# Second feed-forward of a two-layer fp32 backbone: first products of the inner tiles 4 to 21 by Strassen's seven block products

## The chip, the core and the metric

One core of one Trainium2 chip runs the whole kernel as one launch. The metric is the device time of a run in microseconds (us), lower is better; the number compared is the median of the runs.

## What is computed

The reference is a backbone of two layers over 512 latent tokens of 1024 channels. The edited part is the feed-forward at the end of the second layer (l = 1), a SwiGLU with 2816 hidden channels:

```
hn  = rms_norm(h) * (1 + scale) + shift        # 512 tokens x 1024 channels
a   = silu(hn @ w1) * (hn @ w3)                # 512 x 2816
h   = h + gate * (a @ w2)                      # 512 x 1024
```

Everything is float32. TensorE multiplies in a shorter form, so each factor x is carried as a high part xh (x rounded to that form) and a low part xl = x - xh, and each product is three matmul passes: xh*yh, xl*yh and xh*yl.

## The kernel before

Channels lie on the 128 partitions, tokens along the free axis. The 2816 hidden channels are 22 tiles of 128 (j = 0 to 21), in three groups, `GROUPS = [(0, 8), (8, 8), (16, 6)]`. `ffn` (L866) does for each group first its tiles and then eight output tiles dt of w2. Tile 0 of a layer comes from `Lead` (L268), begun before the norm is known. For every other tile:

- `Stream.get` (L147) hands out two weight tiles, w1 and w3 of this j, each 128 x 1024 (eight blocks of 128 channels, kt = 0 to 7). `Stream.fill` (L137) loads raw tiles four ahead through SP's queue (`w_r`) and splits them two ahead: ScalarE writes the high part `w_h` (L65, the helper `act`), VectorE the low part `w_l` (L144).
- TensorE runs `passes` (L157 to L161): for each kt and for w1 and w3 three matmuls of 512 columns (all tokens) into the two halves of the PSUM tile `h_ps`: 48 matmuls for a tile. The moving operands `hnh`, `hnl` are the high and low parts of hn, made once from `nrm_u` (L326).
- `si` = Silu of one half (ScalarE), `av` = si times the other half (VectorE, L893), and its split: `ah` (ScalarE), `al` (VectorE, L896).

Then `w_ps`, the product with w2, takes 24 matmuls of 512 columns for a dt (18 in the last group), again in `passes`, and L907 adds it to h. A scheduler sets each engine's order; the PSUM tag of `h_ps` has two slots, the rings of `w_h` and of `w_l` three slots in either of two pools.

Further up in layer 1 the pooling mixer has `z_ps` (L159 to L161 from `pool_z`), a product by matmuls of 256 columns, and `pl_ps` (L996 to L999).

Of the kernel before, what the change touches and what calls it, by code (L numbers as in the profile page):

```python
# [22 lines left out]
GROUPS = [(0, 8), (8, 8), (16, 6)]  # L23
EPS = 1e-6
# [5 lines left out]
def kernel(  # L30
# [92 lines left out]
    class Stream:  # L123
        """Weight tiles in the order of their use: loaded LD tiles and split LS tiles ahead."""

        def __init__(self, units, LD=4, LS=2):
            self.units, self.LD, self.LS, self.raw, self.ready, self.used = units, LD, LS, [], [], 0

        def load(self, n):
            while len(self.raw) < min(n, len(self.units)):  # L130
                src, m = self.units[len(self.raw)]
                self.raw.append(raw_tile(m, "w_r"))
                nc.sync.dma_start(out=self.raw[-1], in_=src)

        def fill(self, used):
            while len(self.ready) < min(used + self.LS, len(self.units)):
                k = len(self.ready)  # L137
                self.load(k + 1)
                n = self.units[k][1]
                pool, t = (wp_, "") if alt["pool"] is None or k % 2 == 0 else (alt["pool"], "2")  # L140
                hi = pool.tile([P, n], F32R, tag="whi" + t, bufs=3, name="w_h")
                act(hi, self.raw[k])
                lo = pool.tile([P, n], F32R, tag="wlo" + t, bufs=3, name="w_l")
                nc.vector.tensor_tensor(lo, self.raw[k], f32(hi), op=ALU.subtract)  # L144
                self.ready.append((hi, lo))
            self.load(used + self.LD)

# [32 lines left out]
    class AdaCols:  # L180
        """Modulation columns [l][t]: each a product with the broadcast condition, summed along the free axis."""
# [24 lines left out]
    class Norm:  # L206
        """Statistics of an RMS norm, one 128-channel tile at a time."""
# [22 lines left out]
        def rstd_cols(self, ps=None):  # L230
            """One column per 128 tokens, which lie on the partitions."""
            if ps is None:
                ps = mm.tile([P, 512], F32, tag="mm", name="nrm_ps")
            nb = self.n // P
            for m, src_ in enumerate(self.parts):
                for b in range(nb):
                    nc.tensor.matmul(ps[:, b:b + 1], src_[:, b * P:(b + 1) * P], ones[:, 0:1],
                                     start=(m == 0 and b == 0), stop=(m == len(self.parts) - 1 and b == nb - 1))
            std = cp.tile([P, nb], F32, tag="stdc", bufs=2, name="std")
            act(std, ps[:, 0:nb], AF.Sqrt, scale=1.0 / D, bias=eps)  # L240
            rs = cp.tile([P, nb], F32, tag="stdc", bufs=2, name="rs")
            nc.vector.reciprocal(out=rs, in_=std)
            return rs
# [80 lines left out]
    def norm_apply(pool, src, n, rstd, A, B, hi, lo, late=None):  # L324
        u = pb.tile([P, n], F32, tag="tmp", bufs=8, name="nrm_u")
# [18 lines left out]
    def ffn_units(l):  # L344
        u = []
        for gi, (j0, nj) in enumerate(GROUPS):
            for j in range(j0, j0 + nj):
                u += [(w1[l, j], 1024), (w3[l, j], 1024)]
            u += [(w2a[l, gi, dt] if gi < 2 else w2b[l, dt], nj * P) for dt in range(KT)]
        return u  # L350
# [7 lines left out]
    # =============== layer 0: mixer ===============  # L358
    with ExitStack() as es:
# [354 lines left out]
        def attn_out(i, jp, st):  # L714
            """Two heads of either kv group on 128 tokens: probabilities turned and multiplied with the values."""
# [200 lines left out]
    bh = pf.tile([P, 4, 536], F32R, tag="bh", bufs=1, name="bh")  # L916
    bl = pf.tile([P, 4, 16], F32R, tag="bl", bufs=1, name="bl")
# [39 lines left out]
    G1 = cp.tile([P, KT], F32, name="G1")  # L957
    nc.vector.tensor_tensor(G1, ada[1][:, 16:24], g_sb[:, 5, :], op=ALU.mult)
    nrm = Norm(pf, T, sq=("sq", 4, "sqa", 1), eng=nc.gpsimd, direct=4)
    # 128 rows of tokens: first and last with the columns up to the middle, inner ones with their 144 columns;  # L960
    # the reciprocal counts are powers of two except at 8 columns on either end, so only those have a low part
    spans = ((0, 0, 256, 0, 0, 0), (3, 256, 512, 136, 504, 8), (1, 120, 264, 392, 0, 0), (2, 248, 392, 392, 0, 0))
    def pool_z(g):
# [5 lines left out]
        for half in range(2):  # L969
# [7 lines left out]
            zh, zl = sf("zh", dt=F32R, tag="a", bufs=24), sf("zl", dt=F32R, tag="a", bufs=24)  # L977
# [42 lines left out]
    rstd = ffn(1, rstd, Af1, lead).rstd()  # L1020

# [8 lines left out]
def _host_layout(i):  # L1030
# [48 lines left out]
    # constants of the shapes alone  # L1079
# [46 lines left out]
```

## Time and profile before

| | |
|---|---|
| device time, median of 3 runs | 1021.93 us (1021.84 to 1022.23) |
| span of the profiled execution (its own time, first to last instruction) | 1020.0 us |
| median less that span | 1.9 us |
| mean granted TensorE clock | 0.995 of 2.4 GHz |
| tile 1 of layer 1's feed-forward starts on TensorE | 651.2 us |
| DMA, mean over the span | 136 GB/s |

The page gives busy time by engine and by slice of the span; the trace gives every instruction with its start and length. The start of a matmul is recorded, its end is modelled, so the pace of TensorE is read from start to start. Of layer 1's feed-forward, tiles 1 to 7 lie at 651.2 to 729, the first group's w2 to 773.5, tiles 8 to 15 to 862, the second w2 to 906.5, tiles 16 to 21 to 973 and the last w2 behind them.

### The profile page before, as it was taken

To read this page: it belongs to the slowest core of one execution; us is meant where nothing else is said; L and a number is where in the kernel's file an instruction comes from. 1 tells how busy PE (TensorE), PEld (TensorE's weight loads), DVE (VectorE), ACT (ScalarE), POOL (GpSimd) and SP (SyncE) were. 2 spreads that over 40 slices of the span, in tenths; PEclk is the share of its full clock that TensorE was granted. 3 is DMA by queue.
4 is the path that set the end of the run, shared out by engine and by line. 5 is a ranking of instruction groups with operands and counts; after the bars stand their busy time and mean duration, and the time that the engine had idled before them with its cause. 6 is when DMAs were issued, how large, how long until landed. Compare 5 with 4: busy or idle time off the path is not lost.

```text
span 1020.0 us, 12270 instructions
## 1 busy us (share of the span) xinstructions
PE 987.0 (97%) x4816; PEld 783.4 (77%) x4816; DVE 571.5 (56%) x903; ACT 375.3 (37%) x595; POOL 26.6 (3%) x27
## 2 busy tenths in 40 slices
PE   5999999999999999999999998999999999999995
PEld 3666777776888888888888888788888888888884
DVE  4678667889866455663554498842332233323234
ACT  4568565455523212322222455532222232213231
POOL 1011001011000000000000001000000000000000
PEclk9999999999999999999999999999999999999998
DMA  9830322653777356673465431133323223322202
GB/s 349 317 103 31 104 63 87 221 168 109 227 245 264 115 176 215 218 235 124 148 214 163 136 104 55 62 92 112 97 92 93 94 83 102 105 83 75 90 1 83
DMA packets 44409, 139.15 MB, mean 136 GB/s; under 512 B 5440, under 2 KB 5568, under 8 KB 44352
## 3 DMA queue, kind: packets, MB, share of 16 engines
q1 hardware_dynamic: 44352, 138.38, 41.5%
q8 instruction: 38, 0.62, 0.3%
q14 instruction: 19, 0.16, 0.0%
HBM read 136.26 MB, written 2.10 MB: 136 GB/s over the span
## 4 chain that ended last, share of the span: by engine, by line
PE 89%; DVE 7%; ACT 2%; issue 1%; DMA 0%; DVEq 0%; SPq 0%; ACTq 0%
PE h_ps L159 16%; PE h_ps L161 16%; PE h_ps L160 16%; PE w_ps L161 8%; PE w_ps L159 8%; PE w_ps L160 8%; PE pv_ps L734 2%; PE t_ps L723 1%; PE mo_ps L159 1%; PE mo_ps L161 1%; PE mo_ps L160 1%; PE s_ps L686 1%; PE s_cx L399 1%; DVE w_l L144 1%; PE s_ps L687 1%
## 5 line engine op out<-in xcount | busy, mean ns | idle before, releaser
L65 ACT ACTIVATE w_h<-w_r 128x1024 fp32r<-128x1024 f32 (+2 forms) x158 | 156.4, 992 | 452.0 <-PE h_ps L161 275.4
L144 DVE TENSOR_TENSOR w_l<-w_r,w_h 128x1024 fp32r<-128x1024 f32 (+2 forms) x158 | 181.1, 1148 | 196.7 <-ACT w_h L65 196.3
L159 PE MATMUL h_ps<-hnh,w_h 128*128 128x512 f32 x672 | 265.5, 395 | 0.0
L161 PE MATMUL h_ps<-hnl,w_h 128*128 128x512 f32 x672 | 264.8, 394 | 0.0
L160 PE MATMUL h_ps<-hnh,w_l 128*128 128x512 f32 x672 | 264.1, 393 | 0.4 <-DVE w_l L144 0.4
L160 PEld LDWEIGHTS h_ps<-hnh,w_l 128*128 128x128 f32 x672 | 126.5, 188 | 30.2 <-DVE w_l L144 0.8
L161 PEld LDWEIGHTS h_ps<-hnl,w_h 128*128 128x128 f32 x672 | 126.2, 188 | 29.9
L159 PEld LDWEIGHTS h_ps<-hnh,w_h 128*128 128x128 f32 x672 | 126.2, 188 | 28.7
L161 PE MATMUL w_ps<-al,w_h 128*128 128x512 f32 x352 | 138.3, 393 | 0.0
L159 PE MATMUL w_ps<-ah,w_h 128*128 128x512 f32 x352 | 138.3, 393 | 0.0
L160 PE MATMUL w_ps<-ah,w_l 128*128 128x512 f32 x352 | 138.2, 393 | 0.0
L198 DVE SCALAR_TENSOR_TENSOR ada_r<-ada_r,condB 128x1024 f32<-128x1024 f32 x80 | 97.6, 1222 | 66.0 <-DMA ada_r<-in_adaR_dram 66.0
L907 DVE SCALAR_TENSOR_TENSOR h<-w_ps,ada,h 128x512 f32<-128x512 f32 x48 | 36.0, 751 | 101.5 <-PE w_ps L161 101.5
L160 PEld LDWEIGHTS w_ps<-ah,w_l 128*128 128x128 f32 x352 | 66.3, 188 | 14.8
L161 PEld LDWEIGHTS w_ps<-al,w_h 128*128 128x128 f32 x352 | 66.2, 188 | 14.8
L159 PEld LDWEIGHTS w_ps<-ah,w_h 128*128 128x128 f32 x352 | 66.2, 188 | 14.7
L65 ACT ACTIVATE ah<-av 128x512 fp32r<-128x512 f32 x44 | 27.8, 632 | 41.5 <-DVE av L893 39.0
L65 ACT ACTIVATE sq<-h 128x512 f32<-128x512 f32 x38 | 23.4, 624 | 30.5 <-DVE h L907 19.8
L896 DVE TENSOR_TENSOR al<-av,ah 128x512 fp32r<-128x512 f32 x44 | 30.2, 686 | 0.7 <-ACT ah L65 0.7
L65 ACT ACTIVATE p<-s_ps,nm 128x512 f32<-128x512 f32 (+1 forms) x32 | 23.6, 737 | 15.2 <-DVE nm L695 15.0
L694 DVE TENSOR_REDUCE mx<-s_ps 128x1 f32<-128x512 f32 (+1 forms) x32 | 24.1, 753 | 8.9 <-PE s_ps L691 8.7
L893 DVE TENSOR_TENSOR av<-si,h_ps 128x512 f32<-128x512 f32 x42 | 28.6, 680 | 0.0
(244 smaller groups left out, 1106.6 us busy)
## 6 DMA issues: line engine op xcount, KB each, us to landing
w_r<-in_w_dram SPq DMA_DIRECT2D x88, 512.0 KB, 3.5
ada_r<-in_adaR_dram SPq DMA_DIRECT2D x80, 512.0 KB, 4.2
w_r<-in_w2a_dram SPq DMA_DIRECT2D x32, 512.0 KB, 4.2
ada_q<-in_adaP_dram SPq DMA_DIRECT2D x32, 256.0 KB, 5.4
w_r<-in_w2b_dram SPq DMA_DIRECT2D x16, 384.0 KB, 3.1
w_r<-in_wo_dram SPq DMA_DIRECT2D x16, 256.0 KB, 2.8
wa_r<-in_wa_dram SPq DMA_DIRECT2D x8, 384.0 KB, 5.7
h<-in_xT_dram SPq DMA_DIRECT2D x4, 512.0 KB, 5.4
```

The source lines that it names most:

```text
L65: return nc.scalar.activation(out=out, in_=in_, func=func, **kw)
L144: nc.vector.tensor_tensor(lo, self.raw[k], f32(hi), op=ALU.subtract)
L159: nc.tensor.matmul(acc, wh, mh, start=start, stop=False)
L160: nc.tensor.matmul(acc, wl, mh, start=False, stop=False)
L161: nc.tensor.matmul(acc, wh, ml, start=False, stop=stop)
L198: nc.vector.scalar_tensor_tensor(out=r, in0=r, scalar=1.0, in1=condB, op0=ALU.mult, op1=ALU.mult, accum_out=ada[l][:, t:t + 1])
L399: nc.tensor.matmul(ps[32 * g:32 * g + 32, :], condS[:, kt, :], r[:, k * n:(k + 1) * n], start=(kt < 4), stop=(kt >= 4), tile_position=(0, ...
L694: nc.vector.tensor_reduce(out=mx, in_=sp[:, lo_:hi_], op=ALU.max, axis=AX.X)
L734: nc.tensor.matmul(ops[64 * kv:64 * kv + 64, 0:256], VS[:, kbs[n], kv, :], th[:, 256 * kv:256 * kv + 256], start=(n == 0), stop=(n == N - ...
L893: nc.vector.tensor_tensor(av, si, hp[:, 512:1024], op=ALU.mult)
L896: nc.vector.tensor_tensor(al, av, f32(ah), op=ALU.subtract)
L907: nc.vector.scalar_tensor_tensor(out=h[:, dt, :], in0=acc, scalar=ada[l][:, 40 + dt:41 + dt], in1=h[:, dt, :], op0=ALU.mult, op1=ALU.add)
```

## The change

In layer 1 alone, tiles 4 to 21 (18 tiles) go through a new class, `Quarters`. It takes the product of a tile as one of blocks: the stationary matrix has w1 and w3 as its two rows and the lower and upper 512 channels as its two columns (a11, a12 from w1, a21, a22 from w3); the moving matrix has the two halves of the channels as rows and the two halves of the tokens as columns (b11, b12, b21, b22, read out of `hnh` and `hnl`). Strassen's scheme in Winograd's form gets the four result blocks from seven block products. Below, P1 to P7 are these products in the order of the code:

| | stationary | moving | into |
|---|---|---|---|
| P1 | a11 | b11 | r0 |
| P2 | S1 = a21 + a22 | T1 | r2 |
| P3 | S2 = S1 - a11 | T2 | r1 |
| P4 | S3 = a11 - a21 | T3 | r3 |
| P5 | a12 | b21 | r0, added |
| P6 | a22 | T4 | r3, added |
| P7 | S4 = a12 - S2 | b22 | r2, added |

Each is 4 blocks of channels x 3 passes = 12 matmuls of 256 columns, 84 for a tile in place of 48 of 512. r0 to r3 are the quarters of `h_ps`.

Added per tile: `s_f` holds S1 and S2 (two VectorE steps, L928 and L929) or S3 and S4 (L937, L938); four splits, of S1|S2, of w1 whole (`a1`), of a22 alone (512 wide) and of S3|S4, where before there were two. Behind the products: a copy `x` of r0 (ScalarE), `x` + r1 (L969), `v` = that + r3 (L971), `c_q` = v + r2 (L973), later both other blocks in one step of 512 (L981), two Silus of 256, `av` (L986), `ah` and `al` (L1026). `first` issues S1, S2 and the splits of these and of a1; `second` the split of a22 and S3, S4 with theirs. Both are called for tile j+1 inside `run` of tile j.

Added once: T1 to T4 (`pieces`, L905) in the time of tiles 0 to 3 on VectorE, from the eight `nrm_u` that are now kept: 12 SCALAR_TENSOR_TENSOR and 4 TENSOR_TENSOR of 256, and their splits, 4 ScalarE and 4 VectorE steps of 1024.

Laid out anew: the ring of tag "a" has 21 slots in place of 24 and holds `nrm_u` of layer 1 too; the band constants of the mixer lie in a pool that is closed before layer 1's feed-forward, and the new tiles in one opened there. The splits of a tile go to the two pools of `w_h`, `w_l` in turn: S1|S2 and a22 to one, a1 and S3|S4 to the other, three slots each. The number of DMAs and their sizes stay.

```diff
+QUARTERED = (frozenset(), frozenset(range(4, NHID)))
+NA = 21
...
-    def passes(acc, w, m, start, stop):
+    def passes(acc, w, m, start, stop, shared=False):
...
+        def first(self):
+            r1, r3 = ws.take(2)
+            s12 = self.pool.tile([P, 1024], F32, tag="s", bufs=2, name="s_f")
+            nc.vector.tensor_tensor(s12[:, 0:512], r3[:, 0:512], r3[:, 512:1024], op=ALU.add)
+            nc.vector.tensor_tensor(s12[:, 512:1024], s12[:, 0:512], r1[:, 0:512], op=ALU.subtract)
+            n = dict(r1=r1, r3=r3, f=s12, s12=ws.split(s12), a1=ws.split(r1))
+            self.next = n
+
+        def second(self):
+            n = self.next
+            n["a22"] = ws.split(n["r3"][:, 512:1024])
+            s34 = self.pool.tile([P, 1024], F32, tag="s", bufs=2, name="s_f")
+            nc.vector.tensor_tensor(s34[:, 0:512], n["r1"][:, 0:512], n["r3"][:, 0:512], op=ALU.subtract)
+            nc.vector.tensor_tensor(s34[:, 512:1024], n["r1"][:, 512:1024], n["f"][:, 512:1024], op=ALU.subtract)
+            n["s34"] = ws.split(s34)
...
+        def product(self, acc, w, c0, m, start=False):
+            for k in range(4):
+                s_ = slice(c0 + k * P, c0 + k * P + P)
+                passes(acc, [x[:, s_] for x in w], self.moving(m, k), start and k == 0, k == 3, not start)
+
+        def run(self, more):
+            w = self.next
+            ws.skip(2)
+            hp = ss.tile([P, 1024], F32, tag="s", name="h_ps")
+            r = [hp[:, q * 256:(q + 1) * 256] for q in range(4)]
+            self.product(r[0], w["a1"], 0, "b11", start=True)
+            if more:
+                self.first()
+            else:
+                ws.fill(ws.used)
+            self.product(r[2], w["s12"], 0, "t1", start=True)
+            self.product(r[1], w["s12"], 512, "t2")
+            self.product(r[3], w["s34"], 0, "t3")
+            x = sf("x")
+            act(x[:, 0:256], r[0])
+            nc.vector.tensor_tensor(x[:, 256:512], x[:, 0:256], r[1], op=ALU.add)
+            v = sf("v")
+            nc.vector.tensor_tensor(v[:, 0:256], x[:, 256:512], r[3], op=ALU.add)
+            c = self.pool.tile([P, 768], F32, tag="c", bufs=1, name="c_q")
+            nc.vector.tensor_tensor(c[:, 512:768], v[:, 0:256], r[2], op=ALU.add)
+            if more:
+                self.second()
+            self.product(r[0], w["a1"], 512, "b21")
+            self.product(r[3], w["a22"], 0, "t4")
+            self.product(r[2], w["s34"], 512, "b22")
+            si = sf("si")
+            act(si[:, 0:256], r[0], AF.Silu)
+            nc.vector.tensor_tensor(c[:, 0:512].rearrange("p (a b) -> p a b", a=2),
+                                    x[:, 256:512].unsqueeze(1).broadcast_to([P, 2, 256]),
+                                    hp[:, 512:1024].rearrange("p (a b) -> p a b", a=2), op=ALU.add)
+            act(si[:, 256:512], c[:, 0:256], AF.Silu)
+            av = sf("av")
+            nc.vector.tensor_tensor(av, si, c[:, 256:768], op=ALU.mult)
+            return av
...
+                elif j in quartered:
+                    av = quarters.run(j + 1 in quartered and j + 1 < j0 + nj)
```

The order of the engines, before and now, at two places of the steady part. First VectorE. Before, four steps for a tile (the numbers in the names are buffer numbers; `w_l` is the low part of a weight, `h_ps` a tile's product):

```order
L144 TENSOR_TENSOR w_l_7424<-w_r_7357,w_h_7422 128x1024 [waits DMAHW0_49,Activation_49]
L893 TENSOR_TENSOR av_7347<-si_7345,h_ps_7296 128x512 [waits Activation_49]
L144 TENSOR_TENSOR w_l_7430<-w_r_7363,w_h_7428 128x1024 [waits DMAHW1_49,Activation_49]
L896 TENSOR_TENSOR al_7350<-av_7347,ah_7349 128x512 [waits Activation_49]
L144 TENSOR_TENSOR w_l_7493<-w_r_7426,w_h_7491 128x1024 [waits DMAHW2_49,Activation_49]
L893 TENSOR_TENSOR av_7416<-si_7414,h_ps_7365 128x512 [waits Activation_49]
```

Now, around tile 11's last steps (`h_ps_7090` is tile 11, `h_ps_7218` tile 12, `h_ps_7346` tile 13; `w_l_7166` is of tile 12's S3|S4, `w_l_7236` of tile 13's S1|S2, `w_l_7240` of tile 13's w1, `w_l_7287` of its a22):

```order
L155 TENSOR_TENSOR w_l_7166<-s_f_7161,w_h_7164 128x1024 [waits Activation_49]
L937 TENSOR_TENSOR s_f_7289<-w_r_7086,w_r_7088 128x512 [waits DVE_49]
L155 TENSOR_TENSOR w_l_7236<-s_f_7231,w_h_7234 128x1024 [waits Activation_49]
L981 TENSOR_TENSOR c_q_7155<-x_7150,h_ps_7090 128x512 [waits Activation_49]
L155 TENSOR_TENSOR w_l_7240<-w_r_7086,w_h_7238 128x1024 [waits Activation_49]
L986 TENSOR_TENSOR av_7208<-si_7204,c_q_7155 128x512 [waits Activation_49]
L969 TENSOR_TENSOR x_7278<-x_7278,h_ps_7218 128x256 [waits Activation_49]
L155 TENSOR_TENSOR w_l_7287<-w_r_7088,w_h_7285 128x512
L1026 TENSOR_TENSOR al_7211<-av_7208,ah_7210 128x512 [waits Activation_49]
L971 TENSOR_TENSOR v_7281<-x_7278,h_ps_7218 128x256 [waits DVE_49]
L938 TENSOR_TENSOR s_f_7289<-w_r_7086,s_f_7231 128x512
L973 TENSOR_TENSOR c_q_7283<-v_7281,h_ps_7218 128x256 [waits DVE_49]
```

Fourteen VectorE steps stand for a tile (these twelve and L928, L929 behind them) where four stood, and the low part of tile 13's w1 stands behind two 1024-wide splits and L981.

Then TensorE. Before, a tile's 48 matmuls stand together:

```order
L159 MATMUL h_ps_7227<-hnh_5618,w_h_7151 128x512 [waits Activation_49]
L160 MATMUL h_ps_7227<-hnh_5618,w_l_7153 128x512
L161 MATMUL h_ps_7227<-hnl_5619,w_h_7151 128x512
L159 MATMUL h_ps_7227<-hnh_5618,w_h_7183 128x512 [waits Activation_49]
L160 MATMUL h_ps_7227<-hnh_5618,w_l_7185 128x512
L161 MATMUL h_ps_7227<-hnl_5619,w_h_7183 128x512
```

Now, at the end of P4 of tile 12 and the start of P1 of tile 13:

```order
L181 MATMUL h_ps_7218<-t_h_5751,w_l_7166 128x256
L182 MATMUL h_ps_7218<-t_l_5753,w_h_7164 128x256
L180 MATMUL h_ps_7346<-hnh_5625,w_h_7238 128x256 [waits DVE_49,Activation_49]
L181 MATMUL h_ps_7346<-hnh_5625,w_l_7240 128x256 [waits DVE_49]
L182 MATMUL h_ps_7346<-hnl_5626,w_h_7238 128x256
```

and inside P3 of tile 13, where P5 of tile 12 begins:

```order
L181 MATMUL h_ps_7346<-t_h_5838,w_l_7236 128x256
L182 MATMUL h_ps_7346<-t_l_5840,w_h_7234 128x256
L180 MATMUL h_ps_7346<-t_h_5838,w_h_7234 128x256
L180 MATMUL h_ps_7218<-hnh_5642,w_h_7110 128x256 [waits DVE_49,Activation_49]
L181 MATMUL h_ps_7218<-hnh_5642,w_l_7112 128x256
L182 MATMUL h_ps_7218<-hnl_5643,w_h_7110 128x256
```

Products of two tiles now interleave: from one P5 to the next TensorE runs P5 to P7 of tile j (36 matmuls), the last 5 of P3 and the 12 of P4 of tile j+1, P1 and P2 of tile j+2 (24) and 7 of its P3. The second matmul of P1 waits for `w_l` of w1, the first for `w_h` and for L981 of the tile whose slot of `h_ps` it takes.

## Rows read from the trace of the kernel before

**Rows 1.** The page: busy time of the engines over the span with instruction counts, and the granted TensorE clock in 40 equal slices (tenths, 9 is 90% or more).

```profile
PE 987.0 (97%) x4816; PEld 783.4 (77%) x4816; DVE 571.5 (56%) x903; ACT 375.3 (37%) x595; POOL 26.6 (3%) x27
PEclk9999999999999999999999999999999999999998
```

**Rows 2.** The page: the chain of work that ended last, by engine.

```profile
PE 89%; DVE 7%; ACT 2%; issue 1%; DMA 0%; DVEq 0%; SPq 0%; ACTq 0%
```

**Rows 3.** Windows: the stretch, its length, busy us of PE, PEld, DVE, ACT, POOL with instruction counts, granted clock, DMA share, GB/s. The first lies in the pooling mixer and the end of its norm; the others are tiles 1 to 3, tiles 4 to 7, tiles 8 to 15 and tiles 16 to 21 of layer 1's feed-forward.

```profile
628.00:640.00 12.00, 10.14 (x90) 8.30 (x90) 12.00 (x20) 8.16 (x13) 1.34 (x1) 1.00 0.13 38
651.20:684.50 33.30, 33.30 (x145) 27.02 (x146) 16.43 (x21) 13.44 (x20) 0.00 (x0) 1.00 0.30 95
684.50:729.00 44.50, 44.50 (x193) 36.08 (x192) 14.25 (x16) 12.47 (x17) 0.00 (x0) 1.00 0.30 95
773.50:862.00 88.50, 88.50 (x384) 71.74 (x383) 26.90 (x30) 22.95 (x29) 0.00 (x0) 1.00 0.28 90
906.50:973.00 66.50, 66.50 (x289) 53.91 (x288) 18.71 (x22) 15.92 (x22) 0.00 (x0) 1.00 0.23 72
```

**Rows 4.** Timeline of TensorE in tile 4: start, length, instruction. The second row is the 24th matmul behind the first.

```profile
694.24 0.40 PE L161 MATMUL h_ps<-hnl,w_h 128*128 128x512 f32 x1
...
699.80 0.40 PE L161 MATMUL h_ps<-hnl,w_h 128*128 128x512 f32 x1
```

**Rows 5.** Timeline of TensorE in `z_ps` of the pooling mixer, matmuls of 256 columns; the second row is the 32nd behind the first.

```profile
611.41 0.28 PE L159 MATMUL z_ps<-w_h,pxh 128*128 128x256 f32 x1
...
615.24 0.28 PE L161 MATMUL z_ps<-w_l,pxh 128*128 128x256 f32 x1
```

**Rows 6.** The weight loads of the same stretch.

```profile
611.41 0.19 PEld L160 LDWEIGHTS z_ps<-w_h,pxl 128*128 128x128 f32 x1
611.53 0.19 PEld L161 LDWEIGHTS z_ps<-w_l,pxh 128*128 128x128 f32 x1
```

**Rows 7.** Timeline of VectorE at the end of tile 3: start, length, instruction, in brackets the idle time before it and what ended it.

```profile
685.34 1.23 DVE L144 TENSOR_TENSOR w_l<-w_r,w_h 128x1024 fp32r<-128x1024 f32 x1 [7.57 <-ACT w_h L65]
686.48 0.68 DVE L893 TENSOR_TENSOR av<-si,h_ps 128x512 f32<-128x512 f32 x1
687.08 1.22 DVE L144 TENSOR_TENSOR w_l<-w_r,w_h 128x1024 fp32r<-128x1024 f32 x1
688.21 0.69 DVE L896 TENSOR_TENSOR al<-av,ah 128x512 fp32r<-128x512 f32 x1
```

**Rows 8.** Timeline of ScalarE in the same stretch.

```profile
684.24 1.06 ACT L65 ACTIVATE w_h<-w_r 128x1024 fp32r<-128x1024 f32 x1 [7.55 <-PE h_ps L161]
685.21 0.58 ACT L65 ACTIVATE si<-h_ps 128x512 f32<-128x512 f32 x1
685.68 1.06 ACT L65 ACTIVATE w_h<-w_r 128x1024 fp32r<-128x1024 f32 x1
687.19 0.64 ACT L65 ACTIVATE ah<-av 128x512 fp32r<-128x512 f32 x1 [0.45 <-DVE av L893]
```

**Rows 9.** Groups of instructions by form: steps of VectorE and ScalarE of 256 and 512 columns, their count, busy us and mean ns, and the idle time before them.

```profile
L896 DVE TENSOR_TENSOR al<-av,ah 128x512 fp32r<-128x512 f32 x22 | 15.1, 686 | 0.7 <-ACT ah L65 0.7
L749 DVE TENSOR_TENSOR o<-pv_ps,rb 128x256 f32<-128x256 f32 x8 | 3.4, 421 | 3.0 <-ACT rb L65 3.0
L65 ACT ACTIVATE rb<-pv_ps 128x256 f32<-128x256 f32 x8 | 3.1, 382 | 0.0
```

**Rows 10.** Timeline around the end of a product in w2: the last matmul of one `w_ps`, and the first VectorE and ScalarE steps that waited for it.

```profile
740.06 0.40 PE L161 MATMUL w_ps<-al,w_h 128*128 128x512 f32 x1
740.50 0.75 DVE L907 SCALAR_TENSOR_TENSOR h<-w_ps,ada,h 128x512 f32<-128x512 f32 x1 [3.11 <-PE w_ps L161]
740.54 1.06 ACT L65 ACTIVATE w_h<-w_r 128x1024 fp32r<-128x1024 f32 x1 [4.42 <-PE w_ps L161]
```

**Rows 11.** Timeline in the pooling mixer: a VectorE step, the matmul that waited for it, and the next matmul.

```profile
621.39 0.68 DVE L985 TENSOR_TENSOR zl<-z,zh 128x512 fp32r<-128x512 f32 x1
...
622.13 0.39 PE L999 MATMUL pl_ps<-bh,zl 128*128 128x256 f32 x1 [0.46 <-DVE zl L985]
...
622.35 0.23 PE L996 MATMUL pl_ps<-bh,zh 128*128 128x144 f32 x1
```

**Rows 12.** Timeline of VectorE in the first feed-forward's last product: a step and the next, which reads what it wrote.

```profile
585.97 0.28 DVE L280 TENSOR_SCALAR wb<-w_r,ada 128x128 f32<-128x128 f32 x1
586.29 0.35 DVE L282 SCALAR_TENSOR_TENSOR wb<-w_r,ada,wb 128x128 f32<-128x128 f32 x1
```

**Rows 13.** DMA issues: the weights of layer 1's first products, count, KB each, median us from issue to landing.

```profile
w_r<-in_w_dram SPq DMA_DIRECT2D x88, 512.0 KB, 3.5
```

More of the change, by code (lines that the diff above doesn't have):

```diff
@@ L127, in __init__ @@
             self.units, self.LD, self.LS, self.raw, self.ready, self.used = units, LD, LS, [], [], 0
+            self.whole, self.slots = {i for i, u in enumerate(units) if len(u) > 2}, 0
         def load(self, n):
             while len(self.raw) < min(n, len(self.units)):
-                src, m = self.units[len(self.raw)]
+                src, m = self.units[len(self.raw)][:2]
                 self.raw.append(raw_tile(m, "w_r"))
@@ L137, in fill, with split, take, skip @@
                 k = len(self.ready)
+                if k in self.whole:
+                    break
                 self.load(k + 1)
[L139 to L145, printed above, removed]
-            self.load(used + self.LD)
+                self.ready.append(self.split(self.raw[k]))
+            self.load(used + self.LD)
+        def split(self, src):
+            n = src.shape[-1]
+            pool, t = (wp_, "") if alt["pool"] is None or self.slots % 2 == 0 else (alt["pool"], "2")
+            self.slots += 1
+            hi = pool.tile([P, n], F32R, tag="whi" + t, bufs=3, name="w_h")
+            act(hi, src)
+            lo = pool.tile([P, n], F32R, tag="wlo" + t, bufs=3, name="w_l")
+            nc.vector.tensor_tensor(lo, src, f32(hi), op=ALU.subtract)
+            return hi, lo
+        def take(self, n):
+            k = len(self.ready)
+            self.load(k + n)
+            self.ready += [None] * n
+            return self.raw[k:k + n]
+        def skip(self, n):
+            self.used += n
+            self.load(self.used + self.LD)
         def get(self):
@@ L155, in peek @@
             return self.raw[self.used + n]
-    def passes(acc, w, m, start, stop):
+    def passes(acc, w, m, start, stop, shared=False):
         (wh, wl), (mh, ml) = w, m
-        nc.tensor.matmul(acc, wh, mh, start=start, stop=False)
-        nc.tensor.matmul(acc, wl, mh, start=False, stop=False)
-        nc.tensor.matmul(acc, wh, ml, start=False, stop=stop)
+        nc.tensor.matmul(acc, wh, mh, start=start, stop=False, skip_group_check=shared)
+        nc.tensor.matmul(acc, wl, mh, start=False, stop=False, skip_group_check=shared)
+        nc.tensor.matmul(acc, wh, ml, start=False, stop=stop, skip_group_check=shared)
     def ada_load(src, alloc):
@@ L322, in scaled, with norm_apply @@
         nc.vector.scalar_tensor_tensor(out=lo, in0=h_, scalar=a, in1=f32(hi), op0=ALU.mult, op1=ALU.subtract)
-    def norm_apply(pool, src, n, rstd, A, B, hi, lo, late=None):
-        u = pb.tile([P, n], F32, tag="tmp", bufs=8, name="nrm_u")
+    def norm_apply(pool, src, n, rstd, A, B, hi, lo, late=None, u=None):
+        if u is None:
+            u = pb.tile([P, n], F32, tag="tmp", bufs=8, name="nrm_u")
         nc.vector.scalar_tensor_tensor(out=u, in0=src, scalar=A, in1=rstd, op0=ALU.mult, op1=ALU.mult)
@@ L347, in ffn_units @@
             for j in range(j0, j0 + nj):
[L348 removed]
+                whole = (True,) if j in QUARTERED[l] else ()
+                u += [(w1[l, j], 1024) + whole, (w3[l, j], 1024) + whole]
             u += [(w2a[l, gi, dt] if gi < 2 else w2b[l, dt], nj * P) for dt in range(KT)]
@@ L867, in ffn @@
+    def ffn(l, rstd, A, lead, each=None, pool=None):
         nrm = Norm(pf, T)
-        hn, late = [], []
+        hn, late, us = [], [], []
+        quartered = sorted(QUARTERED[l])
         for kt in range(KT):
@@ L897, in ffn @@
                 a.append((ah, al))
+                if quartered and j < quartered[0]:
+                    for _ in range((0, 1, 2, 1)[j]):
+                        next(pieces)
+                    if j + 1 == quartered[0]:
+                        quarters.first()
+                        quarters.second()
                 if l == 0 and j > 1:
@@ L902, in ffn @@
                 wh, wl = ws.get()
+                if j0 + nj in quartered and dt == KT - 2:
+                    quarters.first()
+                if j0 + nj in quartered and dt == KT - 1:
+                    quarters.second()
                 acc = mm.tile([P, 512], F32, tag="mm", name="w2_ps")
@@ L915 @@
     xs, A1, PX = [], [], []
-    bh = pf.tile([P, 4, 536], F32R, tag="bh", bufs=1, name="bh")
-    bl = pf.tile([P, 4, 16], F32R, tag="bl", bufs=1, name="bl")
+    bh = pq.tile([P, 4, 536], F32R, tag="bh", bufs=1, name="bh")
+    bl = pq.tile([P, 4, 16], F32R, tag="bl", bufs=1, name="bl")
     def pool_band_load(g):
@@ L1019 @@
     lead.product()
-    rstd = ffn(1, rstd, Af1, lead).rstd()
+    stage.close()
+    with tc.tile_pool(name="pt8", bufs=1, reuse_waits="tile") as pt8:
+        rstd = ffn(1, rstd, Af1, lead, pool=pt8).rstd()
     for kt in range(KT):
```

52 lines of the change are left out of this document (44 added, 8 removed).

## The prediction

> **What bounds the kernel now.** I read the page's busy times first: TensorE is busy 97% of the span and its clock was granted in full nearly everywhere [rows 1]. The chain that ended last gives TensorE 89% and VectorE 7% [rows 2]. The windows then say it for the place of the change: in tiles 1 to 21 TensorE is busy in every microsecond at clock 1.00 (2.4 GHz), VectorE for 14 to 27 us of stretches of 44 to 88, ScalarE for less, DMA at 0.3 or below [rows 3]. So a matmul less is time gained one for one, as long as VectorE, whose work the change more than doubles, keeps up. The timelines give paces and hand-offs for that.
>
> **What TensorE saves.** In tile 4, 24 matmuls of 512 columns start in 699.80 - 694.24 = 5.56 us, 0.2317 each [rows 4]; 48 make 11.12 a tile. In the pooling mixer 32 matmuls of 256 columns start in 615.24 - 611.41 = 3.83, 0.1197 each [rows 5], in the same three-pass pattern with a new stationary each time. 84 of them make 10.05. Saved: 1.07 a tile, over 18 tiles **19.2 us**. Halving the columns halves the time within 3.4%, so nearly all of the seven eighths (42/48) survives.
>
> **What VectorE gets.** Its steps are paced by start to start: 1.14 for 1024 columns (685.34 to 686.48, though the step lasts 1.23) and 0.60 for 512 (686.48 to 687.08, lasts 0.68) [rows 7]. So a step that is ready begins about 0.085 before the one ahead ends. 256 columns last 0.42 [rows 9], so 0.34 by the same overlap. A tile had 2 x 1.14 + 2 x 0.60 = 3.5; now it has three of 1024, eight of 512 and three of 256: 3.42 + 4.80 + 1.02 = 9.2, and about 9.4 because a step that reads what the one ahead wrote starts 0.04 behind its end (585.97 + 0.28 to 586.29 [rows 12]). That is under the 10.05 of TensorE, with 0.7 to spare. ScalarE: three splits of 1.06, one of 512 and `ah` at 0.64, three steps of 256 at 0.38 [rows 8, 9]: 5.6, no bound by itself.
>
> [...]
>
> **Where TensorE waits.** The spare is in the mean; the order fixes who waits for whom. Hand-offs: a matmul of 256 columns ends 0.28 behind its start [rows 5]; TensorE to VectorE 0.04 (740.46 to 740.50), to ScalarE 0.08 [rows 10]; ScalarE to VectorE 0.04 (684.24 + 1.06 to 685.34) [rows 7, 8]; VectorE to TensorE 0.06 (622.07 to 622.13), and the restart costs 0.10, since the next matmul comes 0.22 later, not 0.12 [rows 11].
>
> Steady part, zero at the first matmul of P5 of tile j. The `w_h` of S3|S4 of tile j+1 takes the slot in which a1 of tile j lies, so it waits for P5's end: last start 11 x 0.1197 = 1.32, end 1.60, ScalarE 1.68 to 2.74. VectorE: `w_l` of it 2.78 to 4.00; L937, which writes the `s_f` that this split read, 4.04; `w_l` of S1|S2 of j+2 4.64; L981 5.78 (its product P7 ended at 4.5); `w_l` of a1 of j+2 6.38 to 7.60. TensorE may use it at 7.66. It gets to that matmul, the second of P1, after 36 + 5 + 12 + 1 = 54 matmuls, at 6.46. So it waits 1.20 and loses 0.10 on restarting: **1.3 us**. The frame is 11.35, longer than the old 11.12: VectorE's chain takes the gain of such a tile and more. Behind it VectorE has `av`, L969, a22's split, `al`, L971, L938 and L973, 3.5 in all, and the next P5 needs the last of them; TensorE has 30 matmuls (3.6) before that P5, so it is just ready, with nothing to spare.
>
> The order is not the same in each tile. Counting the matmuls ahead of P1's second one in each frame:
> - Tiles 13, 14, 15, 21: 54, wait 1.3, together 5.2.
> - Tiles 12, 20: 59, reached at 7.06, wait 0.60 + 0.10, together 1.4.
> - Tiles 10, 18: 68, reached at 8.14, behind 7.66: none.
> - Tiles 7, 11, 19: 49, P1 following P4 without P5 between. Here ScalarE's first Silu waits for P7 (35 x 0.1197 + 0.28 + 0.08 = 4.55), ends 4.93, the `w_h` of a1 ends 5.90, and P1's first matmul waits from 5.75 to 5.96. The second Silu follows at 5.82 to 6.20, `av` at 6.24, and only then `w_l` of a1 at 6.84 to 8.06. TensorE at 8.12 against 5.87: 2.25 and two restarts, 2.45, together 7.3.
> - Tiles 4, 5, 6, 8, 9, 16, 17: prepared during tiles 0 to 3 or under w2, where VectorE is idle most of the time [rows 3]: none.
>
> Sum 13.9. Seven further places hand over tightly (P5 of tiles 4, 7, 8, 16; the start of w2 behind tiles 7, 15, 21, which waits for `ah`, `al` of the last tile): 0 to 3 us, I take two restarts each, 1.4.
>
> **What costs nothing.** T1 to T4: 12 three-operand steps of 0.40 (0.34 from rows 9, and 0.06 more, as 0.75 [rows 10] stands to 0.69 at 512 columns), 4 of 0.34, four splits of 1.14, about 10.7; tile 4's four splits and four sums 6.4, less its old two splits 2.3: 14.8 in all. In tiles 1 to 3 VectorE is idle for 33.3 - 16.4 = 16.9 us [rows 3], which hides it; the last part, S3|S4, is wanted only 36 matmuls (4.3 us) after tile 4's start. If that cover failed, tile 4 would start up to 3 us late, once. DMA: as many transfers of as many bytes, landing in 3.5 us [rows 13] at a share of 0.3. The smaller ring and the moved pools add waits only on tiles long read. Both sides for these together: nothing to 3 us.
>
> **The sum.** -19.2 + 13.9 + 1.4 = -3.9 us. The profiled execution spans 1020.0; the median of the runs is 1021.93, 1.9 more, which lies around the span and stays. 1021.9 - 3.9 = **1018.0 us**. Bounds: with an overlap of VectorE's steps of 0.07 or 0.10 in place of 0.085 the nine waits change by about 0.1 to 0.2 each, 1 to 2 us; the small places 0 to 3; this case alone lies in 1015.0 to 1021.3.
>
> **Rivals.**
> - *VectorE becomes the bound outright (slower).* Five of the 14 new steps wait for an earlier VectorE step; if that, or the pipe, takes the overlap away, a tile costs whole lengths: 3 x 1.22 + 8 x 0.69 + 3 x 0.42 = 10.44. In each frame VectorE also idles some 1.4 us before `w_l` of S3|S4 (it has only L928 and L929, 2 x 0.69, for the 2.78 until that may start). The cycle is then 11.9, 0.78 over the old tile, on the 15 tiles that aren't first of their group: +11.7, less 3 x 1.07 on those, +8.5: 1030. For it: [rows 12], where the second step starts behind the first one's end. Against it: in [rows 7] four steps running overlap, although each takes something of ScalarE. [...] It decides from a chain 0.66 longer on each of the nine waiting tiles (3.9 + 2.0 over 9), where the loss passes 2 us. Chance 0.09.
> - *The same chain somewhat longer (no difference).* 0.35 more on each of nine tiles, for instance four hand-offs at 0.12 rather than 0.04 to 0.08: +3.2, 1021. Those times come from one row each [rows 10, 11]. Chance 0.15, a fifth of it beyond the bound of slower.
> - *The chain doesn't bind (much faster).* If ScalarE's split of S3|S4 needn't wait for P5, or VectorE's order slips past it, the waits mostly go: 1021.9 - 19.2 + 1.4 = 1004. The order of VectorE is fixed, which speaks against. Chance 0.06.
> - *TensorE's clock falls (slower).* It now pauses nine times or more. If after each P1 and P2 (24 matmuls, 2.9 us) ran at 1.2 GHz, that is 9 x 2.9 = 26 more: 1044. Against it: in 12.00 us of the mixer with 10.14 busy, the clock stayed at 1.00 [rows 3]. The Trainium skill, "TensorE: Matmul & The Clock Gate", section "HAM oscillation — how this bites in real kernels", has a matmul loop whose waits between bursts bring the lower clock again and again; no row here shows one of that kind. Chance 0.03.
> - *The change doesn't do what it says: weight loads set the pace (slower).* Each load lasts 0.19; 84 in a row would be 16.0 a tile, +88 in all. [rows 6] show the loads starting every 0.12, one over the other. Chance 0.01.
>
> **How the numbers follow.** The forecast has 0.66. A measurement of this kernel tells about 0.2%, 2.0 us, from no change, so faster is below 1019.9, slower above 1024.0. Of the 0.66, 0.60 lies below 1019.9 and 0.06 between. Faster: 0.60 + 0.06 = 0.66. Same: 0.06 + 0.12 = 0.18. Slower: 0.03 + 0.09 + 0.03 + 0.01 = 0.16. The range leaves out the outright VectorE bound, the clock, the loads and the free chain (0.19 together) and takes in the longer chain and the bounds of the small places: 1014.0 to 1023.5.
>
> **What would show it.** Right: 256-column matmuls of `h_ps` every 0.12; TensorE pausing once a tile in tiles 11 to 15 and 19 to 21, named L181 (P1) released by `w_l` L155, 1.3 us in the steady tiles, over 2 in tiles 7, 11 and 19, none in 8 to 10 and 16 to 18; TensorE's busy share near nine tenths in tiles 12 to 15, where it had all; VectorE's over eight tenths there; tile 4 starting where it did. Wrong: pauses before P5 instead, or over 2 us in every tile (the outright bound), a lower granted clock, matmuls of 256 columns slower than 0.13, or no pauses at all.

## The result and the profile after

The changed kernel runs in 1014.84 us (1013.26 to 1015.19), the kernel before on the same chip in 1022.08: a ratio of 0.9927, interval 0.9913 to 0.9941. The forecast was 1018.0 in a range of 1014.0 to 1023.5. The sign and the range hold; the size is 7.2 us where 3.9 were forecast. What follows shows that most of the 7.2 is not what the forecast counted.

The page of the kernel after, engines, clock and chain, as in [rows 1, 2]:

```profile
PE 969.7 (96%) x5464; PEld 807.5 (80%) x5464; DVE 690.2 (68%) x1104; ACT 419.5 (41%) x671; POOL 26.7 (3%) x27
PEclk9999999999999999999999999999999999999998
PE 84%; DVE 10%; ACT 3%; DMA 1%; issue 1%; SPq 0%; DVEq 0%; ACTq 0%
```

VectorE has 119 us more, TensorE 17 less, and the chain that ended last has moved a little from TensorE to VectorE. The windows of the kernel after, columns as in [rows 3]: tiles 1 to 3, tiles 4 to 7, tiles 8 to 15, tiles 16 to 21, and a short one after a pause in tile 11.

```profile
646.24:680.45 34.21, 34.21 (x158) 28.55 (x158) 32.37 (x50) 18.70 (x26) 0.00 (x0) 1.00 0.19 62
680.45:724.95 44.50, 42.64 (x340) 41.41 (x339) 32.80 (x48) 20.93 (x30) 0.00 (x0) 1.00 0.31 107
765.77:859.47 93.70, 89.08 (x694) 86.50 (x693) 68.26 (x100) 41.78 (x61) 0.00 (x0) 0.98 0.30 96
898.73:969.00 70.27, 67.20 (x521) 65.28 (x520) 48.62 (x72) 30.12 (x45) 0.00 (x0) 0.98 0.26 85
794.50:798.70 4.20, 4.20 (x25) 4.20 (x25) 2.50 (x6) 0.00 (x0) 0.00 (x0) 0.60 0.39 129
```

VectorE fills tiles 1 to 3 and TensorE pays nothing for it, as forecast. From tile 4 on TensorE has gaps, and the clock is below 1.00 in two stretches. The waits of TensorE in the second feed-forward (engine, waiting line, waited-for line: us in total, times, longest):

```profile
PE h_ps L181 <- DVE w_l L155: 9.2, 9, 1.9
```

Nine waits, all of the second matmul of P1 for the low part of w1, as forecast. One of them, at the start of P1 of tile 13, first TensorE, then VectorE (start, length, instruction, idle before):

```profile
816.44 0.28 PE L182 MATMUL h_ps<-t_l,w_h 128*128 128x256 f32 x1
816.81 0.35 PE L180 MATMUL h_ps<-hnh,w_h 128*128 128x256 f32 x1
817.85 0.38 PE L181 MATMUL h_ps<-hnh,w_l 128*128 128x256 f32 x1 [0.69 <-DVE w_l L155]
818.08 0.28 PE L182 MATMUL h_ps<-hnl,w_h 128*128 128x256 f32 x1
```

```profile
812.98 1.22 DVE L155 TENSOR_TENSOR w_l<-s_f,w_h 128x1024 fp32r<-128x1024 f32 x1 [1.81 <-ACT w_h L67]
814.24 0.69 DVE L937 TENSOR_TENSOR s_f<-w_r 128x512 f32<-128x512 f32 x1
814.85 1.22 DVE L155 TENSOR_TENSOR w_l<-s_f,w_h 128x1024 fp32r<-128x1024 f32 x1
815.99 0.68 DVE L981 TENSOR_TENSOR c_q<-x,h_ps 128x512 f32<-128x512 f32 x1
816.58 1.22 DVE L155 TENSOR_TENSOR w_l<-w_r,w_h 128x1024 fp32r<-128x1024 f32 x1
```

The forecast chain had these five steps at 2.78, 4.04, 4.64, 5.78, 6.38 and the matmul at 7.66; from 810.20 they are at 2.78, 4.04, 4.65, 5.79, 6.38 and 7.65. A matmul of 256 columns comes every 0.12, so TensorE lost 0.25 at the first, 0.92 at the second and 0.11 at the third, 1.28 (forecast 1.3).

Now the place where nothing was changed, the first feed-forward. TensorE in its second group, the kernel before, then the kernel after; the second row of each is the 24th matmul behind the first.

```profile
397.63 0.39 PE L160 MATMUL h_ps<-hnh,w_l 128*128 128x512 f32 x1
...
403.18 0.40 PE L160 MATMUL h_ps<-hnh,w_l 128*128 128x512 f32 x1
```

```profile
395.75 0.39 PE L181 MATMUL h_ps<-hnh,w_l 128*128 128x512 f32 x1
...
401.19 0.39 PE L181 MATMUL h_ps<-hnh,w_l 128*128 128x512 f32 x1
```

0.2313 us a matmul before, 0.2267 after, at the same clock, in the same order. Over the whole first feed-forward (its tile 1 to its last w2 matmul) that is 355.5 us before (251.79 to 607.31) and 348.7 after (252.60 to 601.34): **6.8 us come from a stretch that the change's text hardly touches**. The second feed-forward takes 355.1 before (651.26 to 1006.31) and 351.9 after (646.24 to 998.16), 3.1 less. The rest of the span is 2.8 longer, about 0.8 of it in its head, 1.0 in the mixer (whose clock was 0.54 for 3.7 us) and 1.0 at the end; it differs from run to run (309.3 in p1_late below, 310.9 in layout_48, 313.7 in before_pad32, 309.4 before, 312.2 after), so it is not put down to the change. -6.8 - 3.1 + 2.8 = -7.1, the difference of the spans.

### The profile page after: what moved, and what is told of

Same layout as the page of the kernel before. It is cut to its first block, busy times and chain, and to the rows that moved or that the text cites. A ratio compares the mean times of both kernels' runs of the same rounds, so it can differ in the third digit from the quotient of the medians.

```text
span 1012.9 us, 13906 instructions
## 1 busy us (share of the span) xinstructions
PE 969.7 (96%) x5464; PEld 807.5 (80%) x5464; DVE 690.2 (68%) x1104; ACT 419.5 (41%) x671; POOL 26.7 (3%) x27
## 4 chain that ended last, share of the span: by engine, by line
PE 84%; DVE 10%; ACT 3%; DMA 1%; issue 1%; SPq 0%; DVEq 0%; ACTq 0%
PE h_ps L181 14%; PE h_ps L180 14%; PE h_ps L182 14%; PE w_ps L180 8%; PE w_ps L182 8%; PE w_ps L181 8%; DVE w_l L155 4%; PE pv_ps L757 2%; PE t_ps L746 1%; ACT w_h L67 1%; PE mo_ps L180 1%; DMA ada_q<-in_adaP_dram 1%; PE mo_ps L182 1%; PE mo_ps L181 1%; PE s_ps L709 1%
## 5 line engine op out<-in xcount | busy, mean ns | idle before, releaser
L181 PE MATMUL h_ps<-hnh,w_l 128*128 128x512 f32 (+1 forms) x600 | 211.7, 353 | 9.6 <-DVE w_l L155 9.6
L180 PE MATMUL h_ps<-hnh,w_h 128*128 128x512 f32 (+1 forms) x600 | 211.9, 353 | 0.4
L182 PE MATMUL h_ps<-hnl,w_h 128*128 128x512 f32 (+1 forms) x600 | 210.8, 351 | 0.0
L181 PE MATMUL w_ps<-ah,w_l 128*128 128x512 f32 x352 | 136.9, 389 | 0.0
L181 PEld LDWEIGHTS h_ps<-hnh,w_l 128*128 128x128 f32 x600 | 113.5, 189 | 27.0 <-DVE w_l L155 11.8
L180 PE MATMUL h_ps<-t_h,w_h 128*128 128x256 f32 x288 | 82.8, 288 | 0.0
L181 PE MATMUL h_ps<-t_h,w_l 128*128 128x256 f32 x288 | 82.7, 287 | 0.0
L182 PE MATMUL h_ps<-t_l,w_h 128*128 128x256 f32 x288 | 82.5, 287 | 0.0
L67 ACT ACTIVATE w_h<-s_f 128x1024 fp32r<-128x1024 f32 x36 | 38.2, 1061 | 101.0 <-PE h_ps L182 70.9
L181 PEld LDWEIGHTS w_ps<-ah,w_l 128*128 128x128 f32 x352 | 66.1, 188 | 13.5
L155 DVE TENSOR_TENSOR w_l<-s_f,w_h 128x1024 fp32r<-128x1024 f32 x36 | 44.0, 1223 | 43.5 <-ACT w_h L67 43.5
L180 PEld LDWEIGHTS h_ps<-t_h,w_h 128*128 128x128 f32 x288 | 56.7, 197 | 0.0
```

The lines of the kernel that those rows point to most:

```text
L67: return nc.scalar.activation(out=out, in_=in_, func=func, **kw)
L155: nc.vector.tensor_tensor(lo, src, f32(hi), op=ALU.subtract)
L180: nc.tensor.matmul(acc, wh, mh, start=start, stop=False, skip_group_check=shared)
L181: nc.tensor.matmul(acc, wl, mh, start=False, stop=False, skip_group_check=shared)
L182: nc.tensor.matmul(acc, wh, ml, start=False, stop=stop, skip_group_check=shared)
```

## The experiments

Theories: **A**, the faster pace belongs to the memory layout that came with the change, and the seven products by themselves gain little or lose; **B**, it comes from the products or varies from run to run. All times are medians, ratios to the kernel before on the same chip.

**layout_48**: the change without its products.

```diff
-QUARTERED = (frozenset(), frozenset(range(4, NHID)))
+QUARTERED = (frozenset(), frozenset())
...
+    pad = cp.tile([P, 4], F32, name="pad")
+    nc.vector.memset(pad, 0.0)
```

> The change without its seven products: all tiles of layer 1 go through 48 matmuls of 512 columns, but pools, rings and the small software-DMA area are those of the change, and a pad of 16 bytes a partition puts every tile on the address it has in the change (tiles of weights and operands begin 32 bytes past a multiple of 64). Theory A (the faster 512-column pace, 0.2267 us in the change against 0.2302 to 0.2318 before, belongs to where the operands lie, not to the products): 0.2267 from start to start throughout, some 6.8 us less in the first feed-forward and some 6.5 in the second, about 1009 us in all, so that the seven products cost time. Theory B (the pace comes with the products or differs from run to run): about 1022 us, pace 0.231.

1008.5 us, ratio 0.9865 (0.9846 to 0.9883). Its pace in the first feed-forward, as above (the pad's two lines make the change's L181 L183):

```profile
395.56 0.39 PE L183 MATMUL h_ps<-hnh,w_l 128*128 128x512 f32 x1
...
401.00 0.39 PE L183 MATMUL h_ps<-hnh,w_l 128*128 128x512 f32 x1
```

0.2267 in both feed-forwards; the second takes 348.1 us (644.97 to 993.05) against 351.9 with the products. Theory A holds: the layout gains 13.5 us, and the seven products give back 3.8 of it in the second feed-forward. Between the medians it is 6.3, or 4.1 with after_pad32 below in the place of the change; what goes beyond 3.8 lies outside that stretch.

Which part of the layout? Three runs:

**before_pad32**, the kernel before with a pad that moves its tiles by 32 bytes.

```diff
+    pad = cp.tile([P, 8], F32, name="pad")
+    nc.vector.memset(pad, 0.0)
```

> The kernel before with nothing but a pad of 32 bytes a partition ahead of its tiles, so that weights and operands begin 32 bytes past a multiple of 64, as in the change. Theory A in its narrow form (the 32 bytes alone): pace 0.2267, about 1009 us. Theory A in a wide form (the distance of the pools to each other, or the size of the software-DMA area): pace 0.231, 1022 us. Theory B: 1022 us.

1022.29, ratio 1.0005 (0.9993 to 1.0017), pace 0.2318 in w1 and w3: the 32 bytes are not it.

**after_pad32**, the same pad in the change.

> The change with the same pad of 32 bytes, so that its tiles begin at multiples of 64, as in the kernel before. Narrow theory A: the 512-column pace goes back to about 0.231, 6.8 us more in the first feed-forward and 2.9 in the second's tiles 1 to 3 and w2, about 1024 us. Wide theory A and theory B: 1015 us, pace 0.2267.

1012.56, ratio 0.9907 (0.9892 to 0.9922), pace 0.2267. The same answer from the other side. The 2.3 us to the change are in part the clock: it fell behind one pause here, behind two there (second feed-forward 350.5 against 351.9).

**scratch_alone**:

```diff
-    nc = _bacc.Bacc("TRN2", target_bir_lowering=False, num_devices=1)
+    nc = _bacc.Bacc("TRN2", target_bir_lowering=False, num_devices=1, dynamic_dma_scratch_size=1024)
```

> The kernel before with only the software-DMA area cut to 1024 bytes, which moves every tile down by 15360 bytes and keeps them at multiples of 64. Narrow theory A: pace 0.231, 1022 us. If the area itself or the place in the memory matters: pace 0.2267, about 1009 us.

1022.71, ratio 1.0004 (0.9994 to 1.0014), pace 0.2318. Neither the area nor the place in the memory.

The trace of the kernel before has a hint: its w2 products alternate. There `ah`, `al` lie in the second pool (`pf`), and the weights of successive dt lie in the first and the second pool in turn. One dt with its weights in the second pool, then one with them in the first (first matmul, last of 24; twice):

```profile
469.03 0.39 PE L159 MATMUL w_ps<-ah,w_h 128*128 128x512 f32 x1
...
474.25 0.40 PE L161 MATMUL w_ps<-al,w_h 128*128 128x512 f32 x1
474.48 0.41 PE L159 MATMUL w_ps<-ah,w_h 128*128 128x512 f32 x1
...
479.83 0.40 PE L161 MATMUL w_ps<-al,w_h 128*128 128x512 f32 x1
```

23 steps take 5.22 (0.2270) where weights and moving operand share a pool, 5.35 (0.2326) where they don't. In the kernel before the two pools lie 640 bytes off a multiple of 2048 from each other, because `bh` and `bl` (8576 and 256 bytes) sit in the second; the change moves these two out, and the distance becomes a multiple of 2048. Theory C is that this distance sets the pace.

**before_even**:

```diff
-    bl = pf.tile([P, 4, 16], F32R, tag="bl", bufs=1, name="bl")
+    bl = pf.tile([P, 4, 104], F32R, tag="bl", bufs=1, name="bl")
```

with the small software-DMA area, for room.

> The kernel before with the software-DMA area at 1024 bytes (only to make room) and one small tile (bl) padded, so that the pool of the second ring of weights, of ah and al lies a whole multiple of 2048 bytes from that of the first ring and of hnh, hnl; in the kernel before it is 640 bytes off a multiple. Theory C (the slow pace comes from weights and operands that lie off one another by other than a multiple of 2048 bytes): 512-column pace 0.2267 us in both feed-forwards, about 1009 us. Rival (something else of the new layout: the ring of 21, or what was moved out of the pool): pace 0.231, 1022 us.

1007.73, ratio 0.9864 (0.9842 to 0.9887), pace 0.2267 throughout; first and 24th matmul behind it, at the place as above:

```profile
395.41 0.39 PE L160 MATMUL h_ps<-hnh,w_l 128*128 128x512 f32 x1
...
400.85 0.39 PE L160 MATMUL h_ps<-hnh,w_l 128*128 128x512 f32 x1
```

1408 more bytes in a tile, which nobody reads, are worth 14 us.

**layout_48_odd**:

```diff
-QUARTERED = (frozenset(), frozenset(range(4, NHID)))
+QUARTERED = (frozenset(), frozenset())
...
+    odd = pf.tile([P, 160], F32, tag="odd", bufs=1, name="odd")
+    nc.vector.memset(odd, 0.0)
```

> The layout of the change with 48 matmuls a tile everywhere, and a pad of 640 bytes ahead of the second pool, which puts back the distance of the kernel before. Theory C: pace back at 0.231, about 1022 us. Rival: pace 0.2267, about 1008.5 us.

1022.01, ratio 1.0002 (0.9992 to 1.0011), pace 0.2318: all of it is lost again.

```profile
395.65 0.39 PE L181 MATMUL h_ps<-hnh,w_l 128*128 128x512 f32 x1
...
401.22 0.39 PE L181 MATMUL h_ps<-hnh,w_l 128*128 128x512 f32 x1
```

So the distance of the pools is shown as the cause from both sides. That it acts through a matmul's own weights and moving operand is not shown: w2's alternation speaks for it, but w1 and w3 don't fit it alone. There the weights come from the two pools in turn, three matmuls each, while `hnh`, `hnl` lie in the first. Half the matmuls at 0.2270 and half at 0.2326 would give 0.2298; the kernel before has 0.2318, and its matmuls with weights in the first pool took 0.2311, nearly as much as the others (0.2324). So matmuls whose own weights lie at a fast distance are slowed too where they alternate with the others.

**layout_off64, layout_off512, layout_off1024**: the same with `odd` of 16, 128 and 256 floats.

> The layout of the change with 48 matmuls a tile everywhere and the second pool moved by 64 bytes, so that its distance to the first pool is 64 bytes off a multiple of 2048. If any distance off a multiple of 2048 slows the 512-column matmuls: pace 0.230 to 0.232, 1022 us. If only larger ones do: pace 0.2267, 1008.5 us.

> The same with 512 bytes. If any distance off a multiple of 2048 slows: 1022 us. If what counts is the distance within 512 bytes (640 leaves 128): pace 0.2267, 1008.5 us.

> The same with 1024 bytes, half of a moving operand's row. If any distance off a multiple of 2048 slows: 1022 us. If what counts is the distance within 512 or 1024 bytes: pace 0.2267, 1008.5 us.

64 bytes: 1021.56, ratio 0.9994 (0.9983 to 1.0006), pace 0.2322 in w1 and w3, 0.228 in w2. 512 bytes: 1007.22, ratio 0.985 (0.9824 to 0.9875). 1024 bytes: 1008.31, ratio 0.986 (0.9831 to 0.9889); pace 0.2267 in both. So the distances 0, 512 and 1024 are fast, 64 and 640 slow: of the readings in the expectations, the distance within 512 bytes fits. A distance of 256 bytes was not tried, so a rule by 256 would fit as well.

The next two ask where the products lose.

**p1_late**: P1 goes behind P2 and P3.

```diff
-            self.product(r[0], w["a1"], 0, "b11", start=True)
             if more:
                 self.first()
...
             self.product(r[2], w["s12"], 0, "t1", start=True)
-            self.product(r[1], w["s12"], 512, "t2")
+            self.product(r[1], w["s12"], 512, "t2", start=True)
+            self.product(r[0], w["a1"], 0, "b11")
```

> The change with P1 issued behind P2 and P3, so that TensorE comes to the low part of w1 24 matmuls (2.9 us) later. If VectorE's chain up to that low part is what TensorE waits for (13.6 us in nine tiles), these waits go: by the same chain, with the same durations, TensorE then waits 0.1 at the start of a tile and some 0.7 before P5 in six tiles, 4.9 in all, and there are no pauses of 2 us behind which the clock falls: 11 us less than the change, about 1003.5 us. Rival (VectorE's throughput binds, not the order): the waits only move, within 2 us of the change's 1014.8.

1002.90, ratio 0.981 (0.9792 to 0.9828). The waits of TensorE on VectorE in the feed-forward, and the windows of tiles 4 to 7, 8 to 15, 16 to 21:

```profile
PE h_ps L180 <- DVE c_q L973: 3.9, 6, 0.7
```

```profile
680.50:721.60 41.10, 41.10 (x327) 40.13 (x326) 30.77 (x46) 19.34 (x28) 0.00 (x0) 1.00 0.35 116
761.51:850.50 88.99, 86.38 (x690) 84.32 (x689) 68.34 (x100) 42.04 (x61) 0.00 (x0) 1.00 0.30 101
890.41:956.70 66.29, 64.97 (x521) 63.64 (x520) 48.89 (x72) 30.28 (x45) 0.00 (x0) 1.00 0.29 90
```

The nine waits for w1's low part are gone, six smaller ones remain at P5, and the clock stays at 1.00. Same matmuls, same steps, 11.9 us less than the change (9.7 less than after_pad32): order, not VectorE's throughput, was the price. Against layout_48 it is 5.6 less: in this order the products do gain.

**subset9**: products only where TensorE didn't wait.

```diff
-QUARTERED = (frozenset(), frozenset(range(4, NHID)))
+QUARTERED = (frozenset(), frozenset((4, 5, 6, 8, 9, 10, 16, 17, 18)))
```

> The change with the seven products only in tiles 4, 5, 6, 8, 9, 10, 16, 17, 18, the tiles in which TensorE did not wait; the other nine go through 48 matmuls. If a tile without waits gains 48 x 0.2267 - 84 x 0.1199 = 0.81 us against the same layout: 9 x 0.81 = 7.3 less than the layout with 48 matmuls everywhere (1008.5), some 1 us of it lost at hand-overs, about 1002 us. Rival (the products cost time in themselves, by weight loads or their steps): 1008 us or more.

1002.47, ratio 0.9808 (0.9791 to 0.9825). TensorE is busy all of these tiles (40.00 of 40.00 and 85.10 of 85.10):

```profile
680.50:720.50 40.00, 40.00 (x290) 37.75 (x290) 27.43 (x38) 18.10 (x27) 0.00 (x0) 1.00 0.41 132
764.20:849.30 85.10, 85.10 (x493) 75.31 (x492) 39.62 (x50) 30.48 (x42) 0.00 (x0) 1.00 0.35 112
```

A tile without waits does gain; nine of them gain more than eighteen with nine waiting. Both kernels take some 12 us less than the change; their times can't be told apart.

**p1_late_pool**: p1_late with S4 on GpSimd.

```diff
-            nc.vector.tensor_tensor(s34[:, 512:1024], n["r1"][:, 512:1024], n["f"][:, 512:1024], op=ALU.subtract)
+            nc.gpsimd.tensor_tensor(s34[:, 512:1024], n["r1"][:, 512:1024], n["f"][:, 512:1024], op=ALU.subtract)
```

> The change with P1 behind P2 and P3, and S4 (one 512-wide step a tile) on GpSimd instead of VectorE. In p1_late TensorE still waits 0.8 us before P5 in six tiles for L973 at the end of VectorE's chain; a step of 0.60 less in that chain leaves about 0.3 of it: some 4 us less than p1_late (1002.9), about 999 us. The GpSimd step itself (1.34 us for 512 columns in the kernel before) is not waited for. Rival (GpSimd's step slows VectorE's steps beside it, or S4's split now waits for it): 1003 us or more.

1012.16, ratio 0.9892 (0.987 to 0.9914): 9 us more than p1_late, where 4 less were expected. The waits of TensorE on VectorE are now 12.2 us, where p1_late has 3.9:

```profile
PE h_ps L180 <- DVE c_q L981: 7.5, 9, 1.1
PE h_ps L180 <- DVE c_q L973: 4.7, 10, 1.1
```

At one of the nine for L981, GpSimd's step, VectorE's steps beside and behind it, and TensorE's wait:

```profile
802.63 1.68 POOL L938 TENSOR_TENSOR s_f<-w_r,s_f 128x512 f32<-128x512 f32 x1 [10.12 <-DVE w_l L155]
```

```profile
803.07 1.79 DVE L937 TENSOR_TENSOR s_f<-w_r 128x512 f32<-128x512 f32 x1
804.78 0.68 DVE L981 TENSOR_TENSOR c_q<-x,h_ps 128x512 f32<-128x512 f32 x1
805.38 0.68 DVE L928 TENSOR_TENSOR s_f<-w_r 128x512 f32<-128x512 f32 x1
```

```profile
805.51 0.39 PE L180 MATMUL h_ps<-t_h,w_h 128*128 128x256 f32 x1 [0.94 <-DVE c_q L981]
```

L937 takes 1.79 us beside GpSimd's step, in ten of the 18 tiles, and 0.69 in the change; VectorE gave up 0.6 and lost 1.1, L981 behind it comes later, and TensorE waits for it. The rival holds. The trace of the kernel before had it: in the mixer a step L322 of 512 columns took 1.38 beside a GpSimd step (631.01) and 0.75 elsewhere. The Trainium skill, "GPSIMD Engine Reference", section "1. Specifications", says that GpSimd shares its interfaces to the memory with VectorE and contends with VectorE steps of two inputs in SBUF; L937 is one, and the trace agrees (1.79 against 0.69).

## Why the prediction was right, and where not

**TensorE's saving.** 256-column matmuls came every 0.1199 (forecast 0.1197). 18 tiles x 48 x 0.2318 = 200.3 before, 18 x 84 x 0.1199 = 181.3: 19.0 saved, forecast 19.2. Right, against the pace of the kernel before. Only the prediction's remark that nearly all of the seven eighths survives is too kind: an eighth of a tile is 1.39, and 1.07 of it was left.

**The waits.** 2.4 in each of tiles 7, 11, 19; 0.7 in 12 and 20; 1.28 in 13, 14, 15, 21; none in 8 to 10 and 16 to 18: 13.6, forecast 13.9. Right in place, number and size; the rival in which VectorE binds outright did not come, since its steps overlap as in [rows 7].

**The small hand-overs.** About 2.1 us, forecast 1.4, range 0 to 3.

**The clock.** A part of that rival came. Behind the pauses of tiles 11 and 19 (2.1 us each), though not behind that of tile 7, 15 matmuls each came every 0.21 in place of 0.12, and the granted clock was 0.60 in 794.5 to 798.7 (a mean of 2.4 and 1.2 GHz); 2.9 us in all. I gave this 0.03 as a case by itself; it is better a term behind long pauses. The Trainium skill, "TensorE: Matmul & The Clock Gate", section "HAM oscillation — how this bites in real kernels", describes a fall of the clock behind waits of TensorE for DMA; here the waits were for VectorE, and the trace agrees behind two of these three pauses.

**The failed step** is "What costs nothing": the smaller ring and the moved pools were bounded as "nothing to 3 us", a cost only. The layout gave a gain, and no reason had been named that excludes one: 0.2302 to 0.2318 became 0.2267 for every 512-column matmul of both feed-forwards. That is 6.8 us in the first and, for the 144 + 528 matmuls of 512 columns left in the second, 144 x 0.0051 + 528 x 0.0035 = 2.6.

So the second feed-forward comes out: -19.0 + 13.6 + 2.1 + 2.9 - 2.6 = -3.0, measured -3.1. The products' own part of it is -0.4, where the forecast had -3.9; the clock accounts for 2.9 of the difference. And against the layout without products, where a tile of 48 costs 10.88, the saving is only 18 x 0.81 = 14.6, less than the 18.6 of waits, hand-overs and clock: +4.0, measured +3.8. The sign and the range held by luck: the products' own part is about nothing in the old layout by this sum (no run has them there) and a loss in the new one, and a cause that the forecast did not see supplied the gain.

The rows had shown it: [rows 4] give 0.2317, and within the same trace w2 ran at 0.2270 in every other dt. Two paces of one instruction in one trace ask for a reason before either is taken as the unit.

## What to carry to other kernels

Before a change is credited, run its side effects alone: here the pools' layout was worth 13.5 us and the new products, in the order of the change, cost 4 to 6. A fast algorithm with fewer matmuls is bounded by the chain that prepares its operands; put the product whose operand is ready last behind the others, or apply it only where the preparation is hidden. Look at where pools lie: here distances of 0, 512 and 1024 bytes between the pools of weights and moving operands were fast; check the pace of TensorE for two values.

## What the runs showed of the hardware

- A 512-column matmul (fp32 in the short form) starts every 0.2267 us where weights and moving operand lie 0, 512 or 1024 bytes off a multiple of 2048 from each other (layout_48, before_even, layout_off512, layout_off1024), every 0.228 to 0.232 in the mean where some lie 64 or 640 bytes off (layout_off64, layout_48_odd, before). Matmuls of 256 columns ran at 0.1197 to 0.1199 in both kernels. Why the distance counts stays open; no run varied the moving operand's place and the weights' apart from the pool as a whole.
- A VectorE step of 512 columns with two inputs from SBUF takes 1.79 us beside a GpSimd step (p1_late_pool), 0.69 where GpSimd has none; the GpSimd step there takes 1.29 to 2.15, most often 1.68. No row has that step with VectorE idle.
- Behind pauses of 2.1 us the granted clock fell to about half for some 3 us in two of three cases of the change, in one of three of after_pad32; in the feed-forward never behind the pauses of 0.6 to 0.9 us. In the mixer of the change it was 0.54 in 624.6 to 628.3, behind several short pauses of TensorE (1.28 us busy in 622.5 to 624.5), where before it stayed at 1.00. That is not the change's: in the mixer it fell to 0.50 in before_pad32 (634.1 to 637.5) and before_even (622.1 to 625.5) too, and not in layout_48 or p1_late. What decides between these cases stays open.
